# Gate of the first 1024 tokens as seven quadrant products, with the embeddings computed inside the down product

## The chip, the core and the metric

The kernel is one launch on one core of a Trainium2 chip. The core has five engines that run their own instruction streams: TensorE (PE in the profile; PEld is its weight load), VectorE (DVE), ScalarE (ACT), GpSimd (POOL) and SyncE (SP). They meet only through semaphores. SP, ACT and POOL also issue DMA transfers between DRAM and on-chip memory; SPq, ACTq and POOLq name the queues. The metric is the device time of one execution in microseconds.

## The reference, cut to what matters

One layer of a decoder on 2048 tokens of width 1024, all in float32. After attention, pooling groups and their output projection, there follow the gated MLP and the part that this case is about:

```python
hn = _rmsnorm(h, ln_ffn[i])
up = _causal_dwconv(hn @ w_up[i], conv_w[i], conv_b[i])
gate, val = jnp.split(up, 2, axis=-1)
h = h + (jax.nn.silu(gate) * val) @ w_down[i]          # d_ff = 2816
g = jax.nn.sigmoid(_rmsnorm(h, ln_ple[i]) @ w_ple_gate[i])   # 1024 x 1024
h = h + g * (p[i] @ w_ple[i])                          # p: 2048 x 256
...
return _rmsnorm(h, ln_final)
```

## The kernel before

Everything is kept transposed: features on the 128 partitions, tokens along the row, in chunks of 512 tokens (four chunks, `c` = 0 to 3). `h2[j]` in DRAM is the residual after the down product, for the eight feature blocks `j`. A float32 product is made of three matmuls in a 32-bit format of less precision: every operand is split into a high part (a cast on ACT, line 84) and a low part (a subtraction on VectorE or POOL, line 85), and `mm3` (lines 89, 90, 91) multiplies high x high, high x low and low x high into one bank. The low part of a moving operand is `al`, that of a weight the second half of `wu`; line 90 is the matmul that needs `al`, line 91 the one that needs the weight's low part.

**Up stage.** Gate and value of the MLP are made in 44 turns by seven quadrant products in place of eight. At the end of a turn `results` adds and stores to DRAM the operands that the next product needs (`oq`, lines 1458 to 1484, by SP, and by POOL in the last turn), and in eleven of the turns POOL computes four sums of quadrants of `w_down` and stores them (`dd`, lines 1504 to 1511).

**Down stage.** For each half (1024 tokens: two chunks) the product with `w_down` is cut in quadrants: two column halves of the output features, two chunks of tokens, two halves of d_ff. Seven products (`SEQ`) are chained in two sets of four PSUM banks, tags "A" and "B". Each has 11 units; a unit loads a 128x512 piece of a weight (or weight sum) `rw` (line 1686, SP queue) and a 128x512 operand `ra` (line 1688, SP queue), splits both, and runs 4 x 3 = 12 matmuls. `ahead(n + 4)` loads and splits four units ahead; the first five units use buffers of the up stage, and units 5 and on those of the pool `fd`. When a product ends, VectorE adds the banks to `h` tiles (line 1740), which POOL loaded from DRAM (line 1732); finished quadrants are stored as `h2` by ACT's queue and their squares are summed (lines 154, 155).

**Normalization** of a chunk (a row 4 to 7 of `hn2`): sums of squares through TensorE (`st`, line 100), `ms` on ACT (line 108), a power on POOL (line 110), a split and two diagonal tiles `dg` on VectorE (lines 118 to 123), a product that spreads them over the partitions (`bc`, line 137), a copy `inv` on ACT (line 141), and for each of the eight feature blocks a load `nt`, a product with `inv` (161), a gain and cast on ACT (162) and a low part (163). The row of chunk 0 (row 4) is normalized inside the second half of the down stage (`renorm`), that of the others in the final phase (`norm3`).

**Final phase.** Five pieces of tokens: chunks 0, 1, 2 and two halves of chunk 3. Each piece takes for eight `j` the gate product over eight k (`gp`, 24 matmuls per `j`) and the embedding product over two k (`pl`, 6 matmuls per `j`), then sigmoid (ACT, 1838), product and sum (VectorE, 1839, 1840), squares; a final normalization (`one`, `two_`) follows two to four ticks later, inside the next piece. Five of the eight weight rows of `w_gate` are loaded and split at the end of the down stage (`load_w`, line 985, on POOL's queue), three in the final phase (`load_w2`).

**What sets the order.** TensorE runs in the order in which the program is written. The other engines are ordered by a scheduler, which places each instruction by its own estimate of when it can run; once placed, an engine takes its instructions strictly in that order, and one that waits holds all behind it. A `tile` with `bufs=n` is a ring of n buffers: the next writer waits until all readers of the buffer's last content are done. Pools opened one after the other lie one after the other in memory, and where a new pool lies on memory of a closed one, its first writers wait for the last users of that memory.

## Time and profile before

| | before |
|---|---|
| median of 3 runs | 2391.09 us (2390.11 to 2393.58) |
| the profiled execution | 2395.75 us, span 2394.0 us |
| granted TensorE clock, mean | 0.987 |
| busy: PE, DVE, ACT, POOL | 97%, 72%, 47%, 24% |
| down product begins | about 1726 us into the span |
| final phase begins | about 2153 us into the span |

A row of a timeline is the start in us, the duration, the engine, the source line, the operation with the tile written and the tiles read, and in brackets the idle time of the engine just ahead of it with what ended it. A row of a group has the busy time in us and the mean of one in ns, then the idle time ahead of the group. A row of stretches has, for each engine, its busy time and number of instructions in that window, then the granted clock, the share of the DMA engines that is busy and the GB/s. A row of transfers ends with the median time from issue to landing.

### The profile page before, as it was taken

How to read it: one execution, taken by the hardware profiler on the slowest of the kernel's cores; microseconds unless marked ns; L12 is line 12 of the kernel's file. 1: busy time of each engine (PE TensorE's matmuls, PEld its weight loads, DVE VectorE, ACT ScalarE, POOL GpSimd, SP SyncE). 2: the span in 40 equal slices, each digit the busy share in tenths (PEclk: the TensorE clock that was granted, in tenths of full speed). 3: DMA queues.
4: the chain of work that ended last, by engine and by line, in shares of the span. 5: the costliest groups of instructions: out<-in, count | busy, mean ns of one | idle time of the engine just before them, and what ended most of it. 6: DMA issues, size and time to landing. Idle time of an engine off the chain costs nothing.

```text
span 2394.0 us, 32736 instructions
## 1 busy us (share of the span) xinstructions
PE 2320.2 (97%) x11251; PEld 1962.7 (82%) x11251; DVE 1714.3 (72%) x2684; ACT 1123.5 (47%) x2040; POOL 571.1 (24%) x552
## 2 busy tenths in 40 slices
PE   8999999999989989999999999999999999999998
PEld 7888887988868868888887787888878888888888
DVE  6645445888864668999999998777766565755665
ACT  5332234988832245454447353544444444444332
POOL 3322122356620133344430664000020000001000
PEclk9999999999999999999999999999999999999999
DMA  7534436877576664556567787444487776754332
GB/s 232 185 132 164 179 130 248 269 239 241 161 262 216 214 203 144 189 189 207 189 212 246 265 277 248 156 147 146 141 317 254 240 243 204 224 172 154 119 102 93
DMA packets 240550, 475.99 MB, mean 199 GB/s; under 512 B 37472, under 2 KB 63904, under 8 KB 237312
## 3 DMA queue, kind: packets, MB, share of 16 engines
q1 hardware_dynamic: 205040, 394.64, 50.2%
q0 software_dynamic: 15696, 51.49, 6.0%
q10 hardware_dynamic: 19648, 27.77, 3.3%
q8 instruction: 88, 1.44, 0.3%
q14 instruction: 78, 0.64, 0.1%
HBM read 309.14 MB, written 156.79 MB: 195 GB/s over the span
## 4 chain that ended last, share of the span: by engine, by line
PE 78%; DVE 8%; DMA 5%; issue 3%; ACT 1%; POOL 0%; SPq 0%; ACTq 0%; DVEq 0%; POOLq 0%
PE ua L1375 16%; PE uc L1375 8%; PE dn L89 5%; PE dn L90 5%; PE dn L91 5%; PE ub L1375 4%; PE z L91 4%; PE z L89 4%; PE z L90 4%; PE o L91 2%; PE o L89 2%; PE o L90 2%; PE tp L604 2%; PE gp L89 2%; PE gp L91 2%
## 5 line engine op out<-in xcount | busy, mean ns | idle before, releaser
L90 PE MATMUL dn<-al,wu 128*128 128x512 f32 x616 | 240.3, 390 | 3.2 <-DVE al L85 3.2
L89 PE MATMUL dn<-ah,wu 128*128 128x512 f32 x616 | 240.1, 390 | 0.0
L91 PE MATMUL dn<-ah,wu 128*128 128x512 f32 x616 | 239.8, 389 | 0.0
L85 DVE TENSOR_TENSOR al<-ra,ah 128x512 fp32r<-128x512 f32 x154 | 105.9, 690 | 110.0 <-ACT ah L84 107.8
L89 PE MATMUL z<-hnh,wh 128*128 128x512 f32 (+1 forms) x480 | 170.5, 355 | 10.8 <-ACT hnh L252 6.3
L90 PE MATMUL z<-hnl,wh 128*128 128x512 f32 (+1 forms) x480 | 170.3, 355 | 2.3 <-DVE hnl L253 2.0
L91 PE MATMUL z<-hnh,wl 128*128 128x512 f32 (+1 forms) x480 | 170.1, 354 | 2.3 <-POOL wl L85 1.7
L84 ACT CAST ah<-ra 128x512 fp32r<-128x512 f32 x154 | 95.2, 620 | 143.8 <-PE dn L91 124.9
L90 PEld LDWEIGHTS dn<-al,wu 128*128 128x128 f32 x616 | 115.6, 188 | 29.1 <-DVE al L85 5.2
L85 DVE TENSOR_TENSOR wu<-ru,wu 128x1024 fp32r<-128x1024 f32 x88 | 134.7, 1530 | 3.9 <-ACT wu L84 3.9
L89 PEld LDWEIGHTS dn<-ah,wu 128*128 128x128 f32 x616 | 115.6, 188 | 24.3 <-ACT ah L84 0.4
L91 PEld LDWEIGHTS dn<-ah,wu 128*128 128x128 f32 x616 | 115.6, 188 | 24.1
L1375 PE MATMUL ua<-s1h,wu 128*128 128x512 f32 x352 | 116.8, 393 | 4.4 <-ACT ug L1602 4.4
L1375 PE MATMUL ua<-s4h,wu 128*128 128x512 f32 x352 | 117.2, 394 | 2.6 <-ACT uv L1623 2.6
L1375 PE MATMUL uc<-a22h,wu 128*128 128x512 f32 x352 | 116.9, 393 | 2.7 <-DVE uv L1398 2.7
L1375 PE MATMUL ub<-a12h,wu 128*128 128x512 f32 x352 | 115.7, 389 | 1.1 <-ACT a12h L1431 1.1
L1375 PE MATMUL ua<-s2h,wu 128*128 128x512 f32 x352 | 115.8, 390 | 0.8 <-ACT ug L1576 0.7
L1375 PE MATMUL uc<-s3h,wu 128*128 128x512 f32 x352 | 115.7, 389 | 0.0
L1375 PE MATMUL ua<-a11h,wu 128*128 128x512 f32 x352 | 115.5, 389 | 0.0
L155 DVE TENSOR_TENSOR acc<-acc,sq 128x512 f32<-128x512 f32 (+1 forms) x125 | 81.3, 650 | 47.3 <-ACT sq L154 33.8
L85 DVE TENSOR_TENSOR wu<-rw,wu 128x512 fp32r<-128x512 f32 x149 | 101.1, 688 | 18.7 <-ACT wu L84 18.4
L89 PEld LDWEIGHTS z<-hnh,wh 128*128 128x128 f32 x480 | 94.5, 197 | 22.7 <-ACT hnh L252 6.3
(335 smaller groups left out, 6664.8 us busy)
## 6 DMA issues: line engine op xcount, KB each, us to landing
ru<-in_w_up_dram SPq DMA_DIRECT2D x66, 512.0 KB, 4.2
wr<-in_w_in_dram SPq DMA_DIRECT2D x64, 256.0 KB, 4.4
rw<-in_w_down_dram SPq DMA_DIRECT2D x61, 256.0 KB, 3.7
nt<-h SPq DMA_DIRECT2D x56, 256.0 KB, 3.9
td<-t SPq DMA_DIRECT2D x22, 512.0 KB, 2.6
t<-td SPq DMA_DIRECT2D x22, 512.0 KB, 3.7
nt<-in_w_down_dram POOLq DMA_DIRECT2D x44, 256.0 KB, 5.4
ra<-oq0s SPq DMA_DIRECT2D x44, 256.0 KB, 4.1
```

Source lines behind the costliest of these rows:

```text
L84: nc.scalar.copy(hi, src)
L85: (low or nc.gpsimd).tensor_tensor(lo, src, fp(hi), op=ALU.subtract)
L89: nc.tensor.matmul(ps, wh, ah, start=first, stop=False, skip_group_check=again)
L90: nc.tensor.matmul(ps, wh, al, start=False, stop=False, skip_group_check=again)
L91: nc.tensor.matmul(ps, wl, ah, start=False, stop=last, skip_group_check=again)
L155: nc.vector.tensor_tensor(acc[:, :n], acc[:, :n], sq[:, :n], op=ALU.add)
L604: nc.tensor.transpose(st.tp[:, bs], st.ee[:, bs], g.ident)
L1375: nc.tensor.matmul(pst, x[:, ksl], y, start=first and k == 0 and n == 0, stop=k == HK - 1 and n == 2, skip_group_check=True)
```

## The change

- **Weight sums.** The function that made the sums of `w_down`'s quadrants (`down_sums`, now `weight_sums`) also runs in four further turns of the up stage, for `w_gate`; the sums go to DRAM as `gd`.
- **Embeddings.** The products `pl` of chunks 0 and 1 move into the first half of the down stage, after units 23, 26, 29 and 31 (third product, units q = 1, 4, 7, 9): 96 matmuls with the banks of the other tag. ACT copies the result, POOL's queue stores it as `pe`. Their weights and tokens are loaded on POOL's queue.
- **Operands.** Row 4's `renorm` in the second half is replaced by `gate_operands`: the normalized `h` of chunks 0 and 1 and the sums of its quadrants are formed on VectorE and stored as `og`.
- **Gate stage.** 28 further units (154 to 181; seven products of four units) run through the same loop's machinery: `ahead` now splits their weights on POOL and their operands on VectorE. Banks of products that a later one completes are copied by ACT (`r`); the later one adds on VectorE and takes the sigmoid on ACT; `gated` then multiplies by `pe`, adds to `h` and sums squares. `wanted` loads `pe` and `h`. Row 6's normalization (chunk 2) is made inside this stage.
- **Final phase.** Only chunk 2 and the halves of chunk 3 remain; the final normalizations of chunks 1 and 0 run inside its first piece. The `h` tiles come from a new pool `gk`, opened ahead of `fd` and kept to the end, with 17 buffers for `h` and `h3` together (18 and 11 before).

```diff
+                    if 0 <= q < NP + KD // 2 and slot == 0:
+                        args = (w_down, q, NP, g.dd) if q < NP else (w_gate, q - NP, KD // 2, g.gd)
+                        unit["sum"] = weight_sums(*args)
...
         psd = dctx.enter_context(tc.tile_pool(name="c_psd", bufs=1, space=PSUM, reuse_waits="tile"))
+        gk = ctx.enter_context(tc.tile_pool(name="c_gk", bufs=1, reuse_waits="tile"))
         fd = dctx.enter_context(tc.tile_pool(name="c_fd", bufs=1, reuse_waits="tile"))
+        ectx = ExitStack()
...
+        order += [(2, n, q) for n in range(len(SEQ)) for q in range(KG)]
...
+                nc.sync.dma_start(rw, weights(half, SEQ[x][1], q))
                 ra = fd.tile([P, CH], F32, tag="ra", bufs=4, name="ra")
-                nc.sync.dma_start(ra, g.oq[half][SEQ[x][0]][q])
+                nc.sync.dma_start(ra, (g.og if half == 2 else g.oq[half])[SEQ[x][0]][q])
                 w = wtile()
-                split(nc, w[:, :CH], w[:, CH:], rw, nc.vector)
+                split(nc, w[:, :CH], w[:, CH:], rw, nc.gpsimd if half == 2 else nc.vector)
                 ah = fd.tile([P, CH], F32R, tag="ah", bufs=7, name="ah")
                 al = fd.tile([P, CH], F32R, tag="al", bufs=7, name="al")
                 split(nc, ah, al, ra, nc.vector)
...
+        def embeddings(ep, st, bank_):
+            wp = []
+            for k in range(KP):
+                raw = sb.tile([P, 1024], F32, tag="raw", bufs=2, name="rwp")
+                nc.gpsimd.dma_start(raw, rows(w_ple, k))
...
+            pp = {}
+            def load_p(c):
+                for k in range(KP):
+                    raw = ep.tile([P, CH], F32, tag="nt", bufs=6, name="praw")
+                    nc.gpsimd.dma_start(raw, pT[k, :, c * CH : (c + 1) * CH])
...
+                    split(nc, hi, lo, raw)
+                    pp[c, k] = hi, lo
+            def part(c, grp):
+                for j in range(4 * grp, 4 * grp + 4):
+                    pl = bank_("pl")
+                    for k in range(KP):
+                        mm3(nc, pl, *(w[:, j * P : (j + 1) * P] for w in wp[k]), *pp[c, k], k == 0, k == KP - 1)
+                    out = ep.tile([P, CH], F32, tag="nt", bufs=6, name="pe")
+                    nc.scalar.copy(out, pl)
+                    nc.gpsimd.dma_start(g.pe[j][:, c * CH : (c + 1) * CH], out)
+                if grp == 1 and c == 0:
+                    load_p(1)
+            load_p(0)
+            return part
...
+        def gate_operands(ep, inv):
+            out = []
+            for k in range(KG):
+                t = {}
+                def load(k=k, t=t):
+                    for p, (c, kk) in {"a11": (0, k), "a21": (1, k), "a22": (1, k + KG), "a12": (0, k + KG)}.items():
+                        t[p] = ep.tile([P, CH], F32, tag="nt", bufs=6, name="nt")
+                        nc.gpsimd.dma_start(t[p], g.h2[kk][:, c * CH : (c + 1) * CH])
+                def norm(p, k=k, t=t):
+                    kk = k + KG * (p[2] == "2")
+                    gain = g.vec[:, V_PLE + kk : V_PLE + kk + 1]
+                    nc.vector.scalar_tensor_tensor(t[p], t[p], gain, inv[p[1] == "2"], op0=ALU.mult, op1=ALU.mult)
+                    if p != "a21":
+                        nc.gpsimd.dma_start(g.og[p][k], t[p])
+                def summed(o, dst, x, y, op, k=k, t=t):
+                    t[o] = t[dst]
+                    nc.vector.tensor_tensor(t[o], t[x], t[y], op=op)
+                    nc.gpsimd.dma_start(g.og[o][k], t[o])
+                out.append(load)
+                out += [lambda p=p, f=norm: f(p) for p in ("a11", "a21", "a22", "a12")]
+                out += [
+                    lambda v=v, f=summed: f(*v)
+                    for v in (
+                        ("s1", "a22", "a21", "a22", ALU.add),
+                        ("s3", "a21", "a11", "a21", ALU.subtract),
+                        ("s2", "a11", "s1", "a11", ALU.subtract),
+                        ("s4", "a12", "a12", "s2", ALU.subtract),
+                    )
+                ]
+            return out
...
+        for n, (half, x, q) in enumerate(order[:ndown]):
...
-                ht = fd.tile([P, CH], F32, tag="h", bufs=18, name="h")
+                ht = gk.tile([P, CH], F32, tag="h", bufs=17, name="h")
...
+                ep = ectx.enter_context(tc.tile_pool(name="c_e", bufs=1, side="right", reuse_waits="tile"))
+                embed_part = embeddings(ep, None, other)
...
+            if half == 0 and x == 2 and q in (1, 4, 7, 9):
+                embed_part(*divmod((1, 4, 7, 9).index(q), 2))
...
-                renorm(4, 0, dgs, other)
...
+                    todo.extend(gate_operands(ep, [i for _, i in inv01]))
...
+        def wanted(row, col):
+            for j in range(4):
+                jj = 4 * col + j
+                pe = gr.tile([P, CH], F32, tag="pe", bufs=4, name="pe")
+                nc.gpsimd.dma_start(pe, g.pe[jj][:, row * CH : (row + 1) * CH])
+                ht = gk.tile([P, CH], F32, tag="h", bufs=17, name="h")
+                nc.gpsimd.dma_start(ht, g.h2[jj][:, row * CH : (row + 1) * CH])
+                gts[row, jj] = ht, pe
+        def gated(row, col):
+            if row not in gaccs:
+                gaccs[row] = new_acc() if row else gk.tile([P, CH], F32, tag="gacc", name="gacc")
...
+            for j in range(4):
+                r, (ht, pe) = rs.pop((row, col, j)), gts[row, 4 * col + j]
+                nc.vector.tensor_tensor(r, r, pe, op=ALU.mult)
+                nc.vector.tensor_tensor(ht, ht, r, op=ALU.add)
+                add_square(nc, fd, gaccs[row], ht, fresh and j == 0)
...
+        for n in range(ndown, len(order)):
+            half, x, q = order[n]
+            pa, wb, chain, starts, (row, col) = SEQ[x]
+            mine = "AB"[not chain]
+            if q == 0 and starts:
+                banks[mine] = [psd.tile([P, CH], F32, tag=mine, bufs=4, name="gp") for _ in range(4)]
+            ahead(n + 4)
+            if n >= len(order) - 8 and n % 2 == len(order) % 2 and len(gates) < NW:
+                gates.append(load_w(rows(w_gate, len(gates)), f"g{len(gates)}", nc.vector, nc.gpsimd))
+            if q == 0 and x in (1, 4, 5, 6):
+                wanted(row, col)
+            (wh, wl), (ah, al) = units.pop(n)
+            for j in range(4):
+                js = slice(j * P, (j + 1) * P)
+                mm3(nc, banks[mine][j], wh[:, js], wl[:, js], ah, al, starts and q == 0, q == KG - 1, not starts)
+                if q == KG - 1:
+                    gp = banks[mine][j]
+                    if x in (0, 2, 3):
+                        nc.scalar.copy(rtile(row, col, j), gp)
+                    elif x == 6:
+                        nc.scalar.activation(rtile(row, col, j), gp, AF.Sigmoid)
+                    else:
+                        r = rs[row, col, j]
+                        nc.vector.tensor_tensor(r, r, gp, op=ALU.add)
+                        nc.scalar.activation(r, r, AF.Sigmoid)
+            if q == KG - 1 and x in (1, 4, 5, 6):
+                gated(row, col)
...
+            if x == 2 and q == 0:
+                g.pw[6] = rms_scale(nc, g, psd.tile([P, CH], F32, tag="B", bufs=4, name="st"), acc_of[0])
+            if x == 2 and q == 1:
+                dgs = spread_prep(nc, g, sb, g.pw[6])
+            if x == 2 and q == 3:
+                renorm(6, 2, dgs, lambda name: psd.tile([P, CH], F32, tag="B", bufs=4, name=name))
...
-        pieces = [(c * CH, CH, 0, 4 + c) for c in range(3)] + [(3 * CH, HF, 0, 7), (3 * CH + HF, HF, HF, 7)]
+        pieces = [(2 * CH, CH, 0, 6)] + [(3 * CH, HF, 0, 7), (3 * CH + HF, HF, HF, 7)]
...
+        for x, row in enumerate((1, 0)):
+            hs01 = [gts[row, j][0] for j in range(KD)]
+            tk.later(2 + 2 * x, lambda a=(CH, gaccs[row], hs01, slice(row * CH, (row + 1) * CH), [], hs01): one(*a))
...
-                    whole.append(db.tile([P, CH], F32, tag="h3", bufs=11, name="h3"))
+                    whole.append(gk.tile([P, CH], F32, tag="h", bufs=17, name="h3"))
...
```

The first place is the begin of the down product, on SP. The rows are the last load of the up stage's operands and the first loads in buffers of the pool `fd`; `DMASW` in a wait counts transfers of POOL's queue, `DMAHW` those of SP and ACT, `DVE` and `Pool` instructions of these engines. Before:

```order
L1442 DMA rd_15945<-in_w_down_dram 128x512 [waits DMAHW4_49,DMAHW2_49,DVE_49]
L1686 DMA rw_16043<-in_w_down_dram 128x512 [waits DMAHW3_49]
L1688 DMA ra_16045<-oq0a115_210 128x512 [waits DMASW5_49,DMASW6_49,DMASW4_49,Pool_49]
L1686 DMA rw_16068<-in_w_down_dram 128x512 [waits DMAHW5_49,DMASW6_49]
L1688 DMA ra_16070<-oq0a116_211 128x512 [waits DMAHW6_49]
```

After the change:

```order
L1443 DMA rd_16061<-in_w_down_dram 128x512 [waits DMAHW4_49,DMAHW2_49,DVE_49]
L1693 DMA rw_16162<-in_w_down_dram 128x512 [waits DMAHW1_49,DMAHW3_49,DMASW3_49,DVE_49]
L1695 DMA ra_16164<-oq0a115_210 128x512 [waits DMASW5_49,DVE_49]
L1693 DMA rw_16187<-in_w_down_dram 128x512 [waits DMAHW5_49,DMAHW6_49,DMASW6_49,DMASW1_49]
L1695 DMA ra_16189<-oq0a116_211 128x512
```

Followed to the instructions that raise these counts, the load of `rw_16162` (unit 5) now waits, beside two transfers of SP's own, for VectorE's last but one add of the last turn (line 1481) and POOL's store of `oq1s3`, that of `ra_16164` for the store of `oq1s2` and VectorE's last add (line 1485), that of `rw_16187` (unit 6) for the store of `oq1s4`; before, unit 5's waited for an earlier load and for weight sums of long before.

On ACT at the same place, casts of the first units of `fd` (`wu`, `ah` from `rw`, `ra`) and, after the change, of the embeddings' weights (`wph`) and tokens (`pph`). Before:

```order
L84 CAST wu_15991<-rd_15945 128x512
L84 CAST ah_15994<-ra_15947 128x512
L84 CAST wu_16047<-rw_16043 128x512
L84 CAST ah_16050<-ra_16045 128x512
L84 CAST wu_16072<-rw_16068 128x512
```

After:

```order
L84 CAST wu_16107<-rd_16061 128x512
L84 CAST ah_16110<-ra_16063 128x512
L84 CAST wph_16414<-rwp_16412 128x1024
L84 CAST wph_16420<-rwp_16418 128x1024
L84 CAST pph_16426<-praw_16424 128x512
L84 CAST pph_16432<-praw_16430 128x512
L84 CAST wu_16166<-rw_16162 128x512
L84 CAST ah_16169<-ra_16164 128x512
```

Four casts now stand ahead of those of unit 5; the second weight's load and the tokens' loads are on POOL's queue, the last two behind the last turn's stores.

The second place is the end of the gate stage on VectorE, up to the low part of the last unit (`al_21089`, unit 181) and what follows it; the stage has no counterpart before. `r` are the gate's sums, `pe` the embeddings, `h` the residual, `lg` low parts of the final phase's weights.

```order
L1873 TENSOR_TENSOR r_20621<-r_20621,pe_20954 128x512
L1874 TENSOR_TENSOR h_20952<-h_20952,r_20616 128x512
L1874 TENSOR_TENSOR h_20956<-h_20956,r_20621 128x512
L1873 TENSOR_TENSOR r_20626<-r_20626,pe_20958 128x512
L155 TENSOR_TENSOR acc_20907<-acc_20907,sq_21063 128x512
L1874 TENSOR_TENSOR h_20960<-h_20960,r_20626 128x512
L1873 TENSOR_TENSOR r_20631<-r_20631,pe_20962 128x512
L155 TENSOR_TENSOR acc_20907<-acc_20907,sq_21068 128x512
L1874 TENSOR_TENSOR h_20964<-h_20964,r_20631 128x512
L85 TENSOR_TENSOR al_21089<-ra_21083,ah_21088 128x512
L155 TENSOR_TENSOR acc_20907<-acc_20907,sq_21073 128x512
L85 TENSOR_TENSOR lg2_21095<-rg2_21092,hg2_21094 128x1024
```

The last unit's low part is behind the products and sums of quadrant (1,0), which ends with unit 177. On POOL in that stage, the weights' low parts and the loads of `pe`:

```order
L85 TENSOR_TENSOR wu_20937<-rw_20933,wu_20937 128x512
L985 DMA rg2_21092<-in_w_gate_dram 128x1024
L85 TENSOR_TENSOR wu_20982<-rw_20978,wu_20982 128x512
L85 TENSOR_TENSOR wu_21005<-rw_21001,wu_21005 128x512
L1860 DMA pe_20950<-pe0_447 128x512
L1860 DMA pe_20954<-pe1_448 128x512
L1860 DMA pe_20958<-pe2_449 128x512
L1860 DMA pe_20962<-pe3_450 128x512
L85 TENSOR_TENSOR wu_21034<-rw_21030,wu_21034 128x512
```

Before the change POOL had none of these; the low parts of the down weights are and were VectorE's (`wu` from `rw`).

108 lines of the change are left out of this document (67 added, 41 removed).

## The prediction, on record before the result

> **What bounds the kernel now.** I read the busy times first, then a table of stretches from the start of the down product to the end, then the waits of TensorE.
>
> ```profile
> PE 2320.2 (97%) x11251; PEld 1962.7 (82%) x11251; DVE 1714.3 (72%) x2684; ACT 1123.5 (47%) x2040; POOL 571.1 (24%) x552
> ...
> core 0: us, PE busy (x) PEld busy (x) DVE busy (x) ACT busy (x) POOL busy (x), PEclk, DMA share, GB/s
> 1745.00:1770.00 25.00, 24.56 (x105) 19.15 (x104) 11.91 (x19) 8.75 (x15) 9.14 (x17) 1.00 1.00 372
> 1770.00:2100.00 330.00, 330.00 (x1465) 273.40 (x1464) 213.01 (x341) 162.91 (x287) 9.82 (x16) 1.00 0.74 237
> 2153.00:2330.00 177.00, 176.94 (x822) 147.59 (x820) 107.73 (x166) 61.47 (x100) 14.32 (x11) 1.00 0.39 130
> ...
> PE dn L90 <- DVE al L85: 3.2, 4, 1.8
> ```
>
> TensorE is busy for 330.00 of 330.00 us in the down product and 176.94 of 177.00 in most of the final phase, at full clock; VectorE is busy for 65% and 61% there. So a matmul taken out of these stretches is worth its whole spacing, but only while operands still arrive on time; every late operand is paid in full, for TensorE has no idle time to pay with. The only visible waits, 3.2 us, are at the start of the down product, where the DMA share is 1.00.
>
> **What the change removes.** The matmuls are 0.39 us long but overlap; the spacing is read from their starts.
>
> ```profile
> 2169.73 0.39 PE L89 MATMUL gp<-hnh,hwg 128*128 128x512 f32 x1
> 2170.41 0.39 PE L89 MATMUL gp<-hnh,hwg 128*128 128x512 f32 x1
> ```
>
> Three matmuls in 0.68 us is 0.227 each. Two ordinary chunks of the gate are 2 x 8 x 8 x 3 = 384 matmuls; seven quadrant products are 7 x 4 x 4 x 3 = 336. The 96 of the embeddings are moved, not removed. 48 x 0.227 = **10.9 us off**. All other steps can only take from that.
>
> **Start of the down product.** The first lookahead units 5 to 8 are what keeps TensorE going when the up stage ends.
>
> ```profile
> 1723.78 0.45 SPq L1686 DMA_DIRECT2D rw<-in_w_down_dram  x1
> 1736.10 0.61 ACT L84 CAST wu<-rw 128x512 fp32r<-128x512 f32 x1
> 1742.49 0.69 DVE L85 TENSOR_TENSOR al<-ra,ah 128x512 fp32r<-128x512 f32 x1
> 1743.23 0.50 PE L90 MATMUL dn<-al,wu 128*128 128x512 f32 x1 [1.04 <-DVE al L85]
> 1741.54 0.54 POOL L1458 DMA_DIRECT2D oq1s<-x  x1 [2.12 <-DVE x L1480]
> 1742.26 0.54 POOL L1458 DMA_DIRECT2D oq1s<-yg  x1 [0.19 <-issue]
> 1744.34 2.17 POOL L1732 DMA_DIRECT2D h<-h  x4 [1.54 <-DMA oq1s<-x]
> 1745.72 0.69 DVE L85 TENSOR_TENSOR al<-ra,ah 128x512 fp32r<-128x512 f32 x1 [1.95 <-DMA oq1s<-yg]
> ...
> h<-h POOLq DMA_DIRECT2D x18, 256.0 KB, 7.7
> ra<-oq0a SPq DMA_DIRECT2D x16, 256.0 KB, 5.4
> ```
>
> Before, unit 5's weight load leaves at 1723.78, its cast is done by 1736.7, and TensorE already waits 1.04 us for its `al`. In the changed order (the SP rows shown above) these loads carry waits on the last turn's stores and VectorE adds: the load of `ra` of unit 5 stands behind the store issued at 1741.54, which has landed by about 1744.3 (it releases POOL at 1744.34), and unit 6's behind the one issued at 1742.26, landed by 1745.7. With 5.4 us to landing, `ra` of unit 5 is there at about 1750; 0.61 for its cast and 0.69 for its low part make 1751.3, against 1743.2. ACT adds a second queue: four casts of the embeddings' operands stand ahead, the last two on transfers that leave behind the store of 1742.26. Thus **+8 us**; units 6 to 8 follow with 2.7 us more each. Bounds: +5 with a landing of 2.8 us, the time from the store at 1741.54 to POOL's release; +11 with 7.7, the figure of the POOL queue's loads in this window (1722 to 1775). What is late next are the 16 h loads of the same moment, which before met a DMA share of 1.00; I add nothing, since lookahead refills at one unit in 2.7 us.
>
> **Embeddings and operands inside the down product.** VectorE is 65% busy there, ACT 49%, so the 32 operations for the gate operands (16 scalings, 16 sums, 22 us at 0.69, in place of 16 of a renorm), the casts and the copies hide. One place is tight: the second chunk's embeddings load tokens only after the first chunk's stores on the POOL queue, and have three units, 8.2 us, for a landing of 5.4 to 7.7, a cast of 0.62 and two POOL splits of 1.6 each: 9.2 to 11.5. I take **+2** (0 to 4). The four further weight sums of the up stage are of the kind that eleven turns already carry without a wait at TensorE: 0; without that cover, each would be four POOL operations of about 1.4 us.
>
> **The gate stage: VectorE and POOL.** Here POOL makes the low parts of the weights, 28 subtractions, while VectorE does everything else. The profile has a stretch with such a pairing, the weight sums of the up stage.
>
> ```profile
> 1120.46 0.68 DVE L85 TENSOR_TENSOR wu<-t,wu 128x512 fp32r<-128x512 f32 x1
> 1101.12 1.77 DVE L85 TENSOR_TENSOR wu<-t,wu 128x512 fp32r<-128x512 f32 x1
> ...
> 1114.67 1.29 POOL L1072 TENSOR_TENSOR t<-ru 128x512 f32<-128x512 f32 x1 [9.45 <-DVE wu L85]
> 1100.19 2.15 POOL L1074 TENSOR_TENSOR ru<-ru,t 128x512 f32<-128x512 f32 x1
> ...
> 1080.00:1300.00 220.00, 220.00 (x973) 182.21 (x972) 208.71 (x219) 113.05 (x142) 73.74 (x39) 1.00 0.64 212
> ...
> L85 DVE TENSOR_TENSOR wu<-ru,wu 128x1024 fp32r<-128x1024 f32 x24 | 40.2, 1674 | 0.0
> L85 DVE TENSOR_TENSOR wu<-t,wu 128x512 fp32r<-128x512 f32 x12 | 18.0, 1502 | 0.0
> L85 DVE TENSOR_TENSOR wu<-t,wu 128x1024 fp32r<-128x1024 f32 x11 | 13.4, 1220 | 0.0
> L1389 DVE SCALAR_TENSOR_TENSOR yv<-uv,vec,yv 128x1022 f32<-128x1022 f32 x12 | 19.0, 1587 | 0.4
> L1389 DVE SCALAR_TENSOR_TENSOR yg<-ug,vec,yg 128x1022 f32<-128x1022 f32 x11 | 14.1, 1283 | 0.4
> ```
>
> One and the same subtraction takes 0.68 us with POOL idle and 1.77 with POOL in an operation of its own, and POOL's goes from 1.29 to 2.15. Groups: 24 x (1674 - 1220) = 10.9 us, 12 x (1502 - 680) = 9.9, 12 x (1587 - 1283) = 3.6; 24.4 us of VectorE lost to the 39 POOL operations, 0.63 each, with VectorE 95% busy. The Trainium skill, "SBUF — State Buffer", section "Who interferes with whom", says why: a VectorE operation with two inputs in SBUF and a GpSimd one that reads SBUF take an exclusive lock, and the second waits for the whole of the first. The trace agrees (1.77 is 0.68 and nearly all of a 1.29); by that rule alone every POOL split could cost VectorE its full length, which is the third rival.
>
> Now the sum. From the end of unit 161 to the start of unit 181, the last, are 19 units of 12 matmuls: 19 x 2.72 = 51.7 us. The VectorE order has 80 operations between the add that follows unit 161 and the low part `al` of unit 181: 68 plain ones of 128x512, 8 of L163, 2 of 128x1024, 2 tiny.
>
> ```profile
> 1746.33 0.69 DVE L85 TENSOR_TENSOR wu<-rw,wu 128x512 fp32r<-128x512 f32 x1
> 1746.93 0.69 DVE L85 TENSOR_TENSOR al<-ra,ah 128x512 fp32r<-128x512 f32 x1
> L163 DVE SCALAR_TENSOR_TENSOR hnl<-nt,vec,hnh 128x512 fp32r<-128x512 f32 x24 | 17.2, 747 | 2.3 <-ACT hnh L162 2.3
> L161 DVE TENSOR_TENSOR nt<-nt,inv 128x512 f32<-128x512 f32 x24 | 16.0, 688 | 6.2 <-DMA nt<-h 6.1
> L85 POOL TENSOR_TENSOR wl<-wr,wh 128x512 fp32r<-128x512 f32 x32 | 42.3, 1336 | 77.7 <-ACT wh L84 77.4
> ```
>
> Back to back they stand 0.60 to 0.61 apart: 68 x 0.61 + 8 x 0.68 + 2 x 1.16 + 0.2 = 49.4 us. That leaves 2.3 us, before anything waits. Thirteen POOL splits fall into the stretch (the ring of seven lets seven go ahead): 13 x 0.63 = 8.2. The renorm of chunk 2 has two `nt` buffers in this stage and waits for its loads (before, with more cover, 6.1 us over 24 loads): about 3. So the last low part is late by 49.4 + 8.2 + 3 - 51.7 = **+9 us**. Bounds: 0, if neither POOL nor a load costs anything (49.4 is below 51.7); +21, if each of the 13 costs 1.34, the mean of POOL's subtractions in the project stage (13 x 1.34 = 17.4), and the loads 6. Who waits: `al` of units 179 to 181 stands behind the adds, products and squares of quadrant (1,0), and TensorE takes them in order.
>
> **The final phase.** In its first piece the normalization of row 1 is wanted after the sixth k, 17 us in (six k of 2.72 and the sums).
>
> ```profile
> rwg<-in_w_gate_dram SPq DMA_DIRECT2D x3, 512.0 KB, 4.0
> ...
> L85 POOL TENSOR_TENSOR ppl<-praw,pph 128x512 fp32r<-128x512 f32 x6 | 9.5, 1598 | 73.3 <-ACT pph L84 73.3
> L110 POOL TENSOR_TENSOR pw<-ms,mhalf 128x4 f32<-128x4 f32 x4 | 4.4, 1095 | 56.7 <-ACT ms L108 56.7
> L123 DVE TENSOR_TENSOR dg<-ident,ph 128x512 fp32r<-128x512 f32 x6 | 4.1, 686 | 0.0
> L84 ACT CAST hwg<-rwg 128x1024 fp32r<-128x1024 f32 x3 | 3.1, 1047 | 3.6 <-DMA rwg<-in_w_gate_dram 3.6
> L1838 ACT ACTIVATE sg<-gp 128x512 f32<-128x512 f32 x24 | 14.0, 592 | 37.9 <-PE gp L91 30.0 <-DMA out_dram<-h 4.2 <-DVE h L1840 3.7
> ```
>
> Its `ms` stands on ACT behind the cast of weight row 6, whose load waits for VectorE's low part of row 4, itself behind the products, adds and squares of the last quadrant: about 6.5 us into the phase at 0.61 to 1.4 an operation. Then 4.0 us for the load, 1.05 + 0.62 + 0.25 on ACT, POOL's split of 1.60 and its power of 1.10, and two `dg` of 0.69 put `dg` 16.5 to 19 in. **+2** (0 to 5). The second group's sigmoids wait for h3 buffers that the output of row 1 frees, with before 0.9 us of slack: **+1.5** (0 to 2).
>
> **Sum** for the profiled execution, 2395.75 us (span 2394.0 and 1.75 around it): -10.9 + 8 + 2 + 9 + 2 + 1.5 = +11.6, 2407.4 us. The median of the runs shown is 2391.09, 4.7 below that execution; on it, **2402.7 us**.
>
> **Rivals.**
> 1. Everything new hides: VectorE is a third idle in both stages by the table, and DMA moves less than half of the time in the final phase. Then -10.9 with 1 or 2 lost: about 2382. Against it: the new waits of the SP rows are in the program, and 49.4 of 51.7 us leaves no third idle.
> 2. Only the first load wait bites: -10.9 + 8 + 2 + 2 + 1.5 = +2.6, 2394, with the waits for the loads some 2 more: just inside or just outside of no change. For it: VectorE operations that read PSUM (16 in the stage) do not meet POOL, and POOL may fall into VectorE's own gaps.
> 3. The pair excludes each other fully: every split costs 1.34, +18.2 in place of +9 with 3 us of load waits, so about 2412; with the start's +11 as well, 2415. It decides when POOL's splits fall only where VectorE is full, which the cross-waits (ACT's last weight casts stand behind VectorE's sums, POOL behind both) make likely late in the stage.
>
> **Chances.** Forecast 0.47; rival 1 0.13; rival 2 0.20, half of it within 0.2%; rival 3 0.20. A difference under 0.2% (4.8 us) can't be told from no change. Faster 0.13, within 0.2% 0.11, slower 0.76. Low end: rival 1 left out up to half, 2386; high end: rival 3 with its larger start, 2418. The forecast's own range is 2397 to 2411.
>
> **What would show it.** Right: a wait of `dn` for `al` of 5 us or more at about 1743 in the changed profile, with SP's `rw` and `ra` of units 5 to 8 issued after 1741; `al` and L161 rows of over 0.8 us mean in the gate stage beside POOL's subtractions of 1.6 or more; TensorE waiting for `al` in the last four units; a wait of `bc` for `dg` some 17 us into the first piece. Wrong: VectorE rows in the gate stage at 0.69 with gaps between them (rivals 1 and 2), or a TensorE without waits at 1743 (rival 1), or waits in the middle of the down product, which I count nowhere.

## The result, and the profile after

The changed kernel takes **2424.59 us** (median of 4 runs, 2423.61 to 2430.26) against 2390.6 (4 runs, 2388.85 to 2393.58) for the kernel before, measured beside it: ratio 1.0146, 95% interval 1.0127 to 1.0165. Slower, as forecast, but by 34 us and not by 12.

The same table of stretches for the kernel after, cut at its own stages (start of the down product, its first half, its second half, gate stage, first final piece, first 20 us of the two half pieces), and the waits of TensorE from 1700 us on (us in total, times, longest):

```profile
core 0: us, PE busy (x) PEld busy (x) DVE busy (x) ACT busy (x) POOL busy (x), PEclk, DMA share, GB/s
1745.00:1770.00 25.00, 12.81 (x43) 10.07 (x44) 9.21 (x13) 8.93 (x14) 14.92 (x25) 0.66 0.97 360
1770.00:2053.00 283.00, 283.00 (x1254) 234.52 (x1254) 163.25 (x255) 137.10 (x242) 26.49 (x46) 1.00 0.77 256
2053.00:2202.00 149.00, 143.54 (x625) 117.64 (x624) 104.35 (x160) 63.84 (x115) 44.32 (x62) 0.98 0.82 282
2202.00:2292.00 90.00, 82.43 (x351) 66.83 (x350) 70.42 (x101) 57.77 (x99) 41.23 (x38) 0.96 0.61 196
2292.00:2350.00 58.00, 57.80 (x264) 47.19 (x263) 42.85 (x66) 21.20 (x33) 5.14 (x4) 1.00 0.69 225
2350.00:2370.00 20.00, 15.99 (x96) 14.70 (x95) 14.56 (x27) 7.66 (x17) 2.79 (x3) 0.74 0.10 31
```
```profile
PE dn L89 <- ACT ah L84: 16.1, 2, 13.2
PE gp L90 <- DVE al L85: 5.1, 1, 5.1
PE dn L90 <- DVE al L85: 4.3, 2, 2.5
PE bc L137 <- DVE dg L123: 3.8, 2, 1.9
PE gp L90 <- DVE hnl L163: 2.7, 2, 1.6
```

Four of the six stretches have a TensorE that is not busy throughout, and exactly these have a granted clock below 1.00. Between them lie 283 us of the down product without loss and the 58 us of the first final piece with hardly any. (One `bc` wait, at the very end, the kernel before has too.)

The ledger, from the first matmuls of each stage in the two traces. The lengths are measured; "expected" is the length before, with 96 x 0.227 = 21.8 us of embeddings moved into the first half of the down product and 10.9 removed.

| stretch | before | expected | after | lost | forecast |
|---|---|---|---|---|---|
| down product, first `dn` to row 4's sums (`st`) | 287.9 | 309.7 | 323.1 | 13.4 | 8 |
| down product, from there to its end | 139.4 | 139.4 | 149.2 | 9.8 | 2 (for the embeddings, which lost nothing) |
| gate stage and first final piece (before: three pieces, embeddings included) | 169.0 | 136.3 | 148.2 | 11.9 | 9 + 3.5 |
| half pieces and tail | 71.6 | 71.6 | 79.7 | 8.1 | 0 |

The sum is -10.9 + 43.2 = +32.3; the spans from the first `dn` on differ by 700.3 - 667.9 = 32.4. Ahead of it lies the up stage: from its first `s2` matmul, with the wait for it, to the first `dn` it takes 863.6 us before and 869.1 after, but between 860 and 870 in the fifteen kernels of this document that order it alike. So the experiments, most of them single executions, are compared by the stretches, and a total only where there are several runs. In the kernels whose edits leave it alone, the first half of the down product takes 322.8 to 324.0 us, the second 146.7 to 149.5, the gate stage 88.3 to 90.0 and the half pieces 77.8 to 79.7; a difference inside these bounds says nothing.

One loss in the up stage is steady. Between 1500 and 1600 us, where the further weight sums run on POOL, before and then after:

```profile
1500.00:1600.00 100.00, 100.00 (x443) 82.81 (x442) 75.72 (x98) 47.56 (x58) 0.00 (x0) 1.00 0.46 151
1500.00:1600.00 100.00, 98.20 (x427) 80.79 (x426) 86.45 (x97) 45.37 (x55) 31.40 (x38) 0.98 0.62 212
```

In all fifteen changed kernels POOL is busy there for 28 to 36 us and TensorE idle for 0.9 to 4.1 us; before, neither. No run leaves these sums out, so it is not shown that they are the cause.

### The profile page after: what moved, and what is told of

It is laid out like the page before. It is cut to its first block, busy times and chain, and to the rows that moved or that the text cites. A ratio compares the mean times of both kernels' runs of the same rounds, so it can differ in the third digit from the quotient of the medians.

```text
span 2428.5 us, 33136 instructions
## 1 busy us (share of the span) xinstructions
PE 2325.3 (96%) x11203; PEld 1961.7 (81%) x11203; DVE 1769.0 (73%) x2726; ACT 1159.6 (48%) x2110; POOL 714.5 (29%) x726
## 4 chain that ended last, share of the span: by engine, by line
PE 67%; DVE 13%; DMA 8%; issue 6%; ACT 2%; POOL 1%; DVEq 0%; ACTq 0%; POOLq 0%; SPq 0%
PE ua L1376 14%; PE uc L1376 7%; PE dn L89 4%; PE dn L90 4%; PE dn L91 4%; PE z L89 4%; PE z L91 4%; PE z L90 4%; PE ub L1376 3%; DVE wu L85 3%; PE o L91 2%; PE o L89 2%; PE o L90 2%; PE tp L604 2%; DMA nt<-h 1%
## 5 line engine op out<-in xcount | busy, mean ns | idle before, releaser
L85 DVE TENSOR_TENSOR al<-ra,ah 128x512 fp32r<-128x512 f32 x182 | 132.7, 734 | 123.5 <-ACT ah L84 123.0
L84 ACT CAST ah<-ra 128x512 fp32r<-128x512 f32 x182 | 112.4, 620 | 172.4 <-PE dn L91 121.6
L84 ACT CAST wu<-rw 128x512 fp32r<-128x512 f32 x177 | 108.0, 617 | 36.8 <-DMA rw<-in_w_down_dram 20.4
L672 POOL TENSOR_TENSOR s<-s,ev 64x512 f32<-64x512 f32 x60 | 76.8, 1287 | 124.4 <-DMA s<-ev 103.5
```

Of the source, the lines that this page charges most:

```text
L84: nc.scalar.copy(hi, src)
L85: (low or nc.gpsimd).tensor_tensor(lo, src, fp(hi), op=ALU.subtract)
L672: sums.later(3, lambda: nc.gpsimd.tensor_tensor(dst[mine], dst[mine], t[mine], op=ALU.add))
```

## The experiments

### The start of the down product

TensorE, SP, ACT and POOL of the kernel after, around the long wait:

```profile
1757.19 0.79 PE L89 MATMUL dn<-ah,wu 128*128 128x512 f32 x1 [13.15 <-ACT ah L84]
```
```profile
1748.44 0.33 SPq L1695 DMA_DIRECT2D ra<-oq0a  x1
```
```profile
1752.18 1.25 ACT L84 CAST pph<-praw 128x512 fp32r<-128x512 f32 x2 [4.96 <-DMA praw<-in_pT_dram]
...
1756.52 0.62 ACT L84 CAST ah<-ra 128x512 fp32r<-128x512 f32 x1 [2.57 <-DMA ra<-oq0a]
```
```profile
1744.57 0.54 POOL L1459 DMA_DIRECT2D oq1s<-x  x1 [2.27 <-DVE x L1481]
...
1745.83 1.10 POOL L1731 DMA_DIRECT2D praw<-in_pT_dram  x2
```

Unit 5's `ra` waits for the last store from `x`, which left POOL at 1744.57; it leaves SP 3.9 us after that, at 1748.44, and lands 8.1 us later; ahead of its casts ACT waited 4.96 us for tokens of the embeddings. Two causes are possible, and they overlap: *memory* (the pool `gk`, opened ahead of `fd`, pushes the first `rw` and `ra` buffers onto the place of `yg` and `x`, which the last turn still stores) and *ScalarE* (the embeddings' casts stand ahead of the units'). Removing the first alone: the down stage's other tiles are allocated first, so that `rw` and `ra` lie beyond the up stage's.

```diff
+        for tag, dt, nb in (("dacc", F32, 2), ("sq", F32, 1), ("dg", F32R, 2), ("inv", F32, 1), ("nt", F32, 2)):
+            fd.tile([P, CH], dt, tag=tag, bufs=nb, name=tag)
         order = [(half, n, q) for half in range(2) ...
```

> Only the layout of the down operands' pool is changed, so that the first buffers of rw and ra no longer lie on memory of the last turn's yg and x; the four casts of the embeddings still stand ahead of unit 5's on ACT. My theory (the loads' wait is what the 13.15 us at unit 5 hang on; ra landed 4.2 us after the token cast was done): SP issues rw and ra of unit 5 at about 1726 again, but ACT reaches unit 5 only after the tokens' cast at about 1752 to 1753, so the wait shrinks from 13.15 to some 10 us. Rival (the loads alone): the wait is gone, al at 1744, about 15 us off the whole time.

Measured: first half 319.7 (after: 323.1). The long wait shrinks and comes earlier:

```profile
1743.82 0.80 PE L89 MATMUL dn<-ah,wu 128*128 128x512 f32 x1 [8.88 <-ACT ah L84]
```
```profile
1742.11 0.62 ACT L84 CAST pph<-praw 128x512 fp32r<-128x512 f32 x1 [1.07 <-DMA praw<-in_pT_dram]
1742.64 0.61 ACT L84 CAST wu<-rw 128x512 fp32r<-128x512 f32 x1
```

Eight of the units' casts then follow without a gap: their loads had left SP by 1720, and ACT stood at the embeddings. Now ScalarE alone, the embeddings' casts placed behind those of the last unit loaded:

```diff
-                embed_part = embeddings(ep, None, other)
+                with tc.issue_after(casts[-1].ins):
+                    embed_part = embeddings(ep, None, other)
```

> Only the place of the embeddings' operands is changed: their four casts are queued on ACT behind the casts of unit 14; the memory of rw and ra is as in the changed kernel. My theory: the loads of unit 5 still wait for the last turn's stores, ra lands at about 1753 to 1756, so the wait at unit 5 stays at 10 to 13 us. Rival (ACT's queue alone): the wait falls under 5 us.

Measured: 324.5, no gain; the wait is 13.98 us. With memory as it is, the loads come late by themselves. Both together:

> Both edits. If each of the two holds unit 5 by itself, only this one removes the wait: under 2 us at unit 5, no matmuls at half clock behind it, about 13 to 15 us off the whole time of the changed kernel, some 2410. If something third holds it (the DMA queues at this moment), a wait of 5 us or more stays.

Measured: 317.7, 5.4 us less and not the 13 to 15 expected. The long wait is gone; waits of 2.0 and 3.4 us are left, at 1733 and 1767. Each hold was enough to make the wait, so each edit alone showed too little. The longer of the two that are left waits for no load. It waits for an `al` that stands on VectorE behind the low parts of the embeddings' weights and four sums of `h`:

```profile
1763.65 2.15 DVE L85 TENSOR_TENSOR wpl<-rwp,wph 128x1024 fp32r<-128x1024 f32 x1
...
1766.33 0.68 DVE L85 TENSOR_TENSOR al<-ra,ah 128x512 fp32r<-128x512 f32 x1
```

So, beside the memory, the embeddings' loads go to SP, and their loads, casts and low parts behind those of later units:

```diff
-                nc.gpsimd.dma_start(raw, rows(w_ple, k))
+                nc.sync.dma_start(raw, rows(w_ple, k))
...
+            if n == 17:
+                with tc.issue_after(casts[-1].ins), tc.issue_after(loads[-1].ins):
+                    embed_part = embeddings(ep, None, other)
```

> The layout edit, and the embeddings' operands loaded on SP's queue behind the loads of unit 10 and cast behind unit 20: 1.5 MB less in flight while units 5 to 14 are loaded. The stretch from the first down matmul to the row 4 sums took 309.7 us by the rows of before plus the 96 moved matmuls, 323.1 in the changed kernel, 317.7 with both edits of the start. If the 1.5 MB and their casts are the third part: 310 to 313. If the h loads alone fill the queues: 317 as with both edits.

Measured: **314.3**, with waits of 1.75 and 1.41 us at the start, as before the change (1.75 and 1.04). Of the 13.4 us lost 8.8 are back; 4.6 remain, 3.8 of them one wait, of the first `pl` at 1798 for a bank that VectorE's sums of `h` read. This edit moves the loads and the work on them together. Its theory was that the 1.5 MB of loads and their casts are the third thing in the way; for the loads the DMA speaks against it. In the 25 us from 17 us behind the first `dn` its share is 0.98 in `start_both` and 0.98 here, and the loads of `ra` that leave from 1740 to 1766 take as long without the embeddings' transfers beside them. Their medians before, after (1742 to 1768) and in `start_late`:

```profile
ra<-oq0a SPq DMA_DIRECT2D x8, 256.0 KB, 10.0
ra<-oq0a SPq DMA_DIRECT2D x8, 256.0 KB, 10.2
ra<-oq0a SPq DMA_DIRECT2D x9, 256.0 KB, 9.8
```

### The second half of the down product

Here the forecast had put nothing. VectorE and ACT of the kernel after, ahead of the two waits of TensorE at 2133 (2.5 us) and 2152 (2.9 us):

```profile
2129.61 0.75 DVE L1765 SCALAR_TENSOR_TENSOR nt<-nt,vec,inv 128x512 f32<-128x512 f32 x1 [6.37 <-DMA nt<-h]
...
2132.63 0.68 DVE L85 TENSOR_TENSOR al<-ra,ah 128x512 fp32r<-128x512 f32 x1
```
```profile
2149.85 1.63 ACTq L1821 DMA_DIRECT2D h<-h  x2
2151.53 0.63 ACT L154 ACTIVATE sq<-h 128x512 f32<-128x512 f32 x1 [5.85 <-DMA rw<-dd10t]
2152.06 1.12 ACT L84 CAST ah<-ra 128x512 fp32r<-128x512 f32 x2
```

VectorE stands 6.37 us at the scaling of a gate operand whose load has not landed, with the next `al` behind it (one more scaling between). VectorE and ACT are far from full there (104 and 64 us of 149). The gate operands share a ring of six buffers `nt` with the embeddings' tiles; the four loads of a group wait for buffers that the stores of the group before still read. Theory: the ring delays the loads. Rival: the DMA is too busy (share 0.82) whatever the ring. A ring of ten of their own:

```diff
-                        t[p] = ep.tile([P, CH], F32, tag="nt", bufs=6, name="nt")
+                        t[p] = ep.tile([P, CH], F32, tag="gn", bufs=10, name="gn")
```

> The gate operands get a ring of ten buffers of their own in place of six shared with the embeddings, so that their loads go out ahead of the stores of earlier ones. If VectorE's wait of 6.4 us for such a load holds up al at 2133: that wait of 2.5 us goes, the stretch from the row 4 sums to the end of the down product takes 145 to 147 us instead of 149.2 (139.4 before). If the DMA queues are simply full there: no change, or the wait appears for ra or rw.

Measured: second half **139.9** in place of 149.2, and the same in all later kernels that have this ring; before it was 139.4. So the loss of this stretch is the ring's, and with it the second wait goes, though what ACT waits for there was not followed further. The DMA is no less busy (the 40 us that hold both waits, a little earlier in this execution):

```profile
2120.00:2160.00 40.00, 40.00 (x179) 33.11 (x178) 28.42 (x46) 22.30 (x40) 3.25 (x6) 1.00 0.96 330
```

The rival falls: at a share of 0.96 TensorE is busy for 40.00 of 40.00 us.

### The gate stage

Groups of VectorE and POOL in the gate stage of the kernel after (2202 to 2292), then three rows around its first wait (`bc` for `dg`, 1.89 us at 2236):

```profile
L85 DVE TENSOR_TENSOR al<-ra,ah 128x512 fp32r<-128x512 f32 x22 | 15.3, 701 | 9.9 <-ACT ah L84 9.7
L161 DVE TENSOR_TENSOR nt<-nt,inv 128x512 f32<-128x512 f32 x8 | 7.7, 976 | 6.6 <-DMA nt<-h 6.1 <-ACT inv L141 0.5
L85 POOL TENSOR_TENSOR wu<-rw,wu 128x512 fp32r<-128x512 f32 x19 | 29.0, 1544 | 15.1 <-ACT wu L84 15.0
```
```profile
2230.43 3.79 POOL L85 TENSOR_TENSOR wu<-rw,wu 128x512 fp32r<-128x512 f32 x3
2229.86 4.40 DVE L118 CAST ph<-pw 128x4 fp32r<-128x4 f32 x1 [0.93 <-POOL pw L110]
2234.18 0.68 DVE L85 TENSOR_TENSOR al<-ra,ah 128x512 fp32r<-128x512 f32 x1
```

A cast of four numbers per partition lasts 4.40 us, until the third of three POOL subtractions that run one after the other is done. But VectorE's own large operations hardly suffer (`al` 701 ns, 680 undisturbed), except the eight of line 161 (976 ns); POOL's do (1544 ns, alone 1.29 us). To measure the exclusion, POOL's subtractions are left out (line 91 then multiplies the weights' high part again):

```diff
+                if half == 2:
+                    nc.scalar.copy(w[:, :CH], rw)
+                else:
+                    split(nc, w[:, :CH], w[:, CH:], rw, nc.vector)
```

> The gate stage leaves out the low parts of its weights (line 91 multiplies the high part again), so POOL has none of its 28 subtractions there. Theory of the prediction (VectorE and POOL exclude each other): the wait of 5.1 us for al in the last units falls to about 1, that of bc for dg (1.9) goes; the stage, 89 us now, takes about 80. Rival (VectorE's own order and the renorm's loads): al still waits 4 us or more, the stage takes 86 or more.

A first execution of this kernel (`no_pool_low`) took 4013.72 us, with a granted clock of 0.55 from about 1200 us on, and says nothing about the stage. Measured in the second: gate stage **83.5** in place of 89.3, between the 80 of the theory and the 86 of its rival. The same groups there, and its wait:

```profile
L161 DVE TENSOR_TENSOR nt<-nt,inv 128x512 f32<-128x512 f32 x8 | 5.4, 690 | 7.1 <-DMA nt<-h 6.6 <-ACT inv L141 0.5
L118 DVE CAST ph<-pw 128x4 fp32r<-128x4 f32 x1 | 0.2, 171 | 0.9 <-POOL pw L110 0.9
```
```profile
PE gp L90 <- DVE al L85: 4.0, 1, 4.0
```

5.8 us are the exclusion's (the forecast had 8.2), and the wait at the last units is still 4.0 of 5.1. Its reason stands in VectorE's order in the kernel after: TensorE stands from 2280.8 to 2285.84, and `al` of the unit it waits for comes behind squares and sums, and these behind products (`r`, line 1873):

```profile
2283.90 0.68 DVE L155 TENSOR_TENSOR acc<-acc,sq 128x512 f32<-128x512 f32 x1
2284.51 0.68 DVE L1874 TENSOR_TENSOR h<-h,r 128x512 f32<-128x512 f32 x1
2285.11 0.68 DVE L85 TENSOR_TENSOR al<-ra,ah 128x512 fp32r<-128x512 f32 x1
```

So a finished quadrant's products are written one unit later, behind the look-ahead:

```diff
             if q == KG - 1 and x in (1, 4, 5, 6):
-                gated(row, col)
+                pend.append((row, col))
...
             ahead(n + 4)
+            if pend:
+                gated(*pend.pop())
```

> The products, sums and squares of a quadrant are written one unit later, so that on VectorE the low part of the last unit's operand stands ahead of those of quadrant (1,0); nothing else. If VectorE's order is what delays the last unit: the wait of 5.1 us for al goes or falls under 1.5, the gate stage takes 83 to 84 instead of 89 us (the wait and the six slow matmuls behind it). If the operand's load or POOL's weight is late anyway: a wait of 3 us or more stays there under another name.

Measured: gate stage 82.3, 7.0 us shorter, and the first final piece 66.1 in place of 58.9, 7.2 longer. Nothing won. The wait for `al` is gone; these stand in its place, in the final piece:

```profile
2292.66 0.50 PE L89 MATMUL gp<-hnh,hwg 128*128 128x512 f32 x1 [2.76 <-ACT hwg L84]
...
2299.08 1.10 PE L137 MATMUL bc<-dg,onesr 128*128 128x512 f32 x2 [1.17 <-DVE dg L123]
```

What was put off at the end of the gate stage is wanted a few us later, for row 1's sums and the last weight rows.

### The half pieces

VectorE, then TensorE, of the kernel after at the start of the half pieces:

```profile
2327.90 5.38 DVE L1969 SCALAR_TENSOR_TENSOR h<-h,vec,inv 128x512 f32<-128x512 f32 x8
...
2344.56 1.49 DVE L161 TENSOR_TENSOR nt<-nt,inv 128x512 f32<-128x512 f32 x2 [4.69 <-DMA nt<-h]
```
```profile
2353.25 0.38 PE L90 MATMUL gp<-hnl,hwg 128*128 128x256 f32 x1 [1.56 <-DVE hnl L163]
2354.99 0.58 PE L90 MATMUL gp<-hnl,hwg 128*128 128x256 f32 x1 [1.12 <-DVE hnl L163]
```

Row 7's normalization, wanted by the half pieces, starts behind the eight scalings of row 0's final one and then waits for its loads. Two theories: the loads `nt`, which SP issues behind those of the `h3` tiles, come late; or VectorE and ACT come late to them. First the loads on POOL's queue:

```diff
-                    nc.sync.dma_start(tmp, g.h2[k][:, t0 : t0 + n])
+                    nc.gpsimd.dma_start(tmp, g.h2[k][:, t0 : t0 + n])
```

> In the final phase the loads of h2 for the normalization of a row go out on POOL's queue instead of SP's, where they stand behind the loads of the h3 tiles that wait for the output's stores. If that queue order makes the half pieces late: the waits for hnl at the first half piece (1.6 and 1.1 us) go, the half pieces take 72 to 74 us instead of 79.7 (71.6 before the change). If VectorE's and ACT's own work is late (the final normalization of rows 1 and 0): 78 or more.

Measured: half pieces 81.2, no gain, the waits for `hnl` and `hnh` 3.0 and 2.0 us. Then row 0's final normalization eight ticks later:

```diff
-            tk.later(2 + 2 * x, lambda a=(CH, gaccs[row], hs01, slice(row * CH, (row + 1) * CH), [], hs01): one(*a))
+            tk.later(2 + 10 * x, lambda a=(CH, gaccs[row], hs01, slice(row * CH, (row + 1) * CH), [], hs01): one(*a))
```

> The final normalization of row 0 (chunk 0) starts at tick 12, in the first half piece, in place of tick 4; nothing else. Now its eight scalings on VectorE (5.4 us) and its output's issues on ACT stand ahead of the normalization of row 7 that the half pieces need. If that is what makes the half pieces late: the waits for hnl (1.6, 1.1), pph and ppl there go, with the matmuls at low clock behind them, and the half pieces take 71 to 74 us instead of 79.7. If the loads of h2 hold them (they did not gain by another queue): 77 or more.

Measured: half pieces **76.6** in place of 79.7, between the 71 to 74 expected and the 77 of the rival; the waits for `hnl` are gone, two others come up, and behind them the matmuls of 256 columns are 0.21 us apart in place of 0.12:

```profile
2351.99 0.38 PE L89 MATMUL pl<-pph,wph 128*128 128x256 f32 x1 [1.08 <-ACT pph L84]
2353.32 0.39 PE L90 MATMUL pl<-ppl,wph 128*128 128x256 f32 x1 [0.94 <-POOL ppl L85]
2354.96 0.41 PE L90 MATMUL gp<-hnl,hg 128*128 128x256 f32 x1
2355.18 0.41 PE L91 MATMUL gp<-hnh,lg 128*128 128x256 f32 x1
```

### Together

The memory order, the late embeddings, the ring of ten and row 0 late in one kernel (`combo`), and the same with the quadrants' products one unit later (`combo_al`):

> Start (layout, late operands), ring of ten for the gate operands, row 0's final normalization late. If the four causes are separate, the gains add: 10 to 12 at the start, 9 in the second half, 6 to 8 in the half pieces: 2396 to 2400 against 2424.6 of the changed kernel, still slower than before (2390.6) by 0.2 to 0.4%, since the gate stage keeps its 9 to 11 us of loss. If one of them only moves a wait: 2404 or more.

> The combination, with the last units' low parts ahead of the quadrant's products. Alone that edit took 7 us off the gate stage and gave 7 back in the first piece of the final phase, where the weights' casts and the normalization of row 1 came late. If VectorE is the bound over both: the same time as the combination, within 3 us. If row 0's later normalization has freed the first piece: 5 us less, level with before.

Measured, against 2392.43 before: `combo` 2406.32 us (10 runs), ratio 1.0059 [1.0042, 1.0076]; `combo_al` 2407.13 (8 runs), 1.0058 [1.0041, 1.0075]. That is above the 2396 to 2400 expected, because the parts were smaller than put in: 8.8 us at the start for 10 to 12, 3 in the half pieces for 6 to 8. Such as they are, the gains add up in their stretches (315.2, 139.9, 89.5, 57.9, 76.5), and the reordering gives back again what it gains (82.3 and 64.7 in place of 89.5 and 57.9). From the first `dn` on `combo` is 679.0 us long against 700.3.

Two questions were left: the half pieces' last 5 us, and whether the exclusion gives back the reordering's gain. For the first, in `combo` the two late casts of tokens were placed ahead of the first piece's last squares (`embed_early`); on this, POOL's subtractions were left out, without and with the reordering. The edit for the casts:

```diff
+                    if grp == 1:
+                        pps[1] = load_pp(1)
                     for j in range(4):
-                        close(4 * grp + j, gps[j], pls[j])
+                        with tc.issue_after(ppc[-1].ins) if grp and j > 1 else ExitStack():
+                            close(4 * grp + j, gps[j], pls[j])
```

> The version with the late operands, the own ring and row 0 normalized later, and in it the two casts of the half pieces' token operands on ScalarE ahead of the last squares and sigmoids of the first piece. In the version without this, TensorE waits 0.7 and 0.9 us for these operands at the start of the half pieces, and the granted clock there is 0.83 for 10 us. Theory (the late casts, with the slower matmuls that follow a wait, are what is left of the loss of the half pieces): their 76.5 us become 72 to 73 (before the change 71.6), and the median falls from 2406.3 to about 2402. Rival (the piece has simply more VectorE work beside it): the two waits go and others come, 75 to 76 us.

> The same, and GpSimd's 28 subtractions of the gate stage left out (the products with the weights' low parts read the high parts, so the same instructions on TensorE, VectorE and ScalarE, and a wrong output). Theory: the gate stage goes from 89.5 to about 83.5 as it did alone, the rest as in the version above; about 2396, still not under the time before the change (2391 to 2392).

> The same without GpSimd's subtractions, and a quadrant's products written one unit later, so that the last units' low parts stand ahead of them on VectorE. Alone this made the gate stage 7 us shorter and the first final piece 7 us longer. If what gave it back is the time that the exclusion takes from VectorE, now both gains stay: gate stage 76 to 77, first piece 58 to 60, about 2390, no slower than before the change. If VectorE's own work in its order gives it back, the gate stage is 76 to 77 and the first piece 64 to 65, about 2396.

The ratios are to 2391.05 us before (15 runs); the three versions have 4, 10 and 6 runs.

| | first half | second half | gate stage | first piece | half pieces | median us | ratio |
|---|---|---|---|---|---|---|---|
| embed_early | 314.5 | 139.9 | 89.6 | 58.1 | 76.0 | 2405.98 | 1.0064 [1.0047, 1.0081] |
| ee_nolow | 315.6 | 139.9 | 83.6 | 57.9 | 74.4 | 2400.76 | 1.0037 [1.0021, 1.0052] |
| ee_al_nolow | 314.6 | 139.9 | 77.6 | 62.7 | 76.3 | 2400.59 | 1.0036 [1.0017, 1.0055] |

The first expectation missed: the waits for `pph` and `ppl` go, and another stands in their place, row 6's sums, which ScalarE now squares later. This row isn't in `combo`:

```profile
PE st L101 <- DVE acc L156: 1.4, 1, 1.4
```

Of the 4.4 us over the 71.6 before, 1.4 are this wait and about 1.6 slower matmuls behind it (16 of them); the rest isn't accounted for. The second: without the exclusion the reordering still takes 6.0 us from the gate stage and gives 4.8 back in the first piece and 1.9 in the half pieces. So mostly it is not POOL; that it is VectorE's own work in those 140 us fits, but no run takes that work away. And without any POOL subtraction in the gate stage, which the computation needs, the change is still 0.4% slower than before. No version beat the kernel before.

Where the rest lies: from the first `dn` on `ee_al_nolow` takes 671.1 us, only 3.2 more than before, while the whole span of the same trace is 8.4 longer and the median 9.5 above. So most of what is left of it seems to lie ahead of the down product, with the further weight sums, where no experiment was made. As that part varies by 10 us from trace to trace, this is a pointer and not a measurement.

## Why the prediction was right and wrong

**Direction: right.** A TensorE without idle time pays for every late operand; it lost four times what the removed matmuls gave.

**"Start of the down product", +8: right mechanism, mis-sized term.** The loads of unit 5 behind the last turn's stores, and ACT's queue as the second hold, are what `start_memory` and `start_both` show. The measured loss is 13.4. The step that failed is the landing: "with 5.4 us to landing" (bounds 2.8 and 7.7) measured 8.1 for unit 5's `ra`. The 5.4 is a median from 1722 to 1775, in which loads that left early (1722 to 1740: median 5.0 us) stand beside those of the moment to which unit 5's load moves (1740 to 1766: 10.0, before the change as after it). What meets a DMA share of 1.00, for which the prediction adds nothing, was in the trace of before. Two smaller parts: the store from `x` left 3.0 us later than before, of which the whole span was 2.1 late by then, and released the load after 3.9 us in place of 2.8. And the first matmuls after the wait ran at half speed, which is in no term. (With a landing of 7.7 the upper bound of its own working is 10.4 and not 11.)

**"Embeddings and operands inside the down product", +2: wrong, and the largest miss beside the half pieces.** The embeddings' tight place cost nothing. But "the 32 operations for the gate operands ... hide" failed: their busy time hides, their loads don't. The forecast compared VectorE's 65% with the work added, and did not ask when the buffers of the six-deep ring come free. An operation that waits for its load in a strict queue holds the low parts behind it. `ring` leaves 0.5 of the 9.8.

**The further weight sums, 0: not borne out.** The eleven turns do not carry theirs "without a wait at TensorE": they run from 1322 to 1490 in the kernel before, and TensorE waits there 2.69 us at 1376 and 2.27 at 1451. Where the four further ones run it waits 1.80 us after the change, at 1530, and not at all before. Some us of the total are probably this; no run separates them.

**"The gate stage", +9, and "the final phase", +2 and +1.5: right in their sum (11.9 against 12.5), by luck in part.** Against its own matmuls (336 x 0.227 + 0.8 + 0.95 for row 6's products = 78) the stage of 89.3 lost 11.3, and the first piece next to nothing: no wait of `bc` in it, no sigmoid late. The exclusion costs 5.8, not 8.2, and shows otherwise than said: the sum of 13 x 0.63 put it on VectorE's large operations, which stay at 0.68 to 0.70 except line 161's, while POOL's lengthen and one tiny cast is held 4.40 us. The renorm's loads hold VectorE for 6.1 us, not for about 3. The wait for the last `al`, "behind the adds, products and squares of quadrant (1,0)", came as told, 5.06 us.

**The half pieces: not in the sum, +8.1.** With two of three full pieces gone, the first piece is the only cover for three normalizations. The forecast followed row 1 and the sigmoids there, and stopped ahead of row 7. `row0_late` gets up to 3 us back (76.6 against 77.8 to 79.7); of what is left part is waits that move from one late operand to the next.

**What it said would prove it wrong** did: "waits in the middle of the down product, which I count nowhere". Rivals 1 and 2 are out. Rival 3 (2412 to 2415) comes nearer in time but not in cause: the exclusion costs 5.8 us, not 18, and most of VectorE's large operations are not lengthened.

## What to carry to other kernels

Where the bounding engine has no idle time, don't cost added work by the busy share of the engine that does it: for every added load find the buffer it lands in, what frees that buffer, and what stands behind the operation that waits for it. Price the load from those that leave at that moment, not from a median over a longer window. A new pool opened ahead of another shifts every buffer of the other onto new neighbours, and so can make a load wait for a stage that it has nothing to do with. When a wait has two causes, taking away one alone shows little; take both, and then each.

## What the runs showed of the hardware

A wait of TensorE can cost more than its length. After the 13.15 us wait matmuls are 0.43 us apart in place of 0.227 until 1763; after the waits of 2.92 and 1.89 us, eleven and seven of them are as slow, though the second wait is short. But after the wait of 2.52 us at 2133 none is, so the length of the wait alone does not tell. What else does is open. Here TensorE, at 2236, and the stretch around it:

```profile
2236.19 1.11 PE L137 MATMUL bc<-dg,onesr 128*128 128x512 f32 x2 [1.89 <-DVE dg L123]
```
```profile
2236.00:2242.00 6.00, 5.70 (x17) 4.31 (x18) 5.53 (x8) 5.34 (x11) 3.87 (x2) 0.72 0.66 209
```

Added up over the timeline from 1700 on, matmuls spaced like this cost some 11 us beyond their full-speed spacing (about 70 of them), and under 2 before the change: of the 43.2 us lost, about a quarter. The Trainium skill, "TensorE: Matmul & The Clock Gate", section "Part 1: The HAM clock gate (the "warmup" mystery)", has the half clock follow an idle window of about 3.4 us; the traces agree on the half speed, but here 1.89 us of waiting were followed by it, for 3.5 us (2237.6 to 2241.1), and 2.52 us were not.

The cast of 128x4 that lasts 4.40 us in place of 0.17 is the other: by its size it is nothing, and the queue behind it (`dg`, for which TensorE waited) paid for three of POOL's subtractions.
